# Dividing the attention output instead of the probabilities: the softmax sums sent as rows through HBM, once for each pair of heads

## The chip, the core and the metric

The kernel runs on one core of a Trainium2 chip. The metric is device time in microseconds (us) from the first to the last instruction of one execution. The engines are TensorE (PE: matmuls and transposes, with the weight loads PEld beside them), VectorE (DVE), ScalarE (ACT), GpSimd (POOL) and SyncE (SP), which here only issues DMAs. Each engine works through its own instructions strictly in order; they meet through semaphores. PE writes to eight PSUM banks; everything else lies in SBUF or in HBM.

## The reference

One layer of a hybrid backbone over 512 latent tokens with a prefix of 256 context tokens, width 1024: a modulated input projection, 16 heads of latent attention beside a two-way Mamba-2 scan (SSD), one output projection over both, then a gated MLP. What the change touches is the attention:

```python
def attend(q_nope, q_rope, k_nope, k_rope, v):
    s = (jnp.einsum("bqhd,bkhd->bhqk", q_nope, k_nope)
         + jnp.einsum("bqhr,bkr->bhqk", q_rope, k_rope)) * ATTN_SCALE
    p = jax.nn.softmax(s.astype(jnp.float32), axis=-1).astype(v.dtype)
    return jnp.einsum("bhqk,bkhd->bqhd", p, v)
...
mix_x = jnp.concatenate([attn_x, ssd_x], axis=-1) @ w_out[l]
```

Each of the 16 heads has 512 queries, 768 keys (latent and context) and values 64 wide. The softmax divides each row of exponentials by its sum; the division may stand before or behind the product with the values, since a sum belongs to one query.

## The kernel before

Every large product is done in fp32r as three products of a rounded high part and a remainder (high by high, high by low, low by high). So each operand is first split: `split` copies it on ACT to the high part (L497) and subtracts on DVE for the low part (L498). Both lines are a helper's and occur everywhere.

**Attention** goes by pairs of heads, eight of them (`pair_of_heads`). For each pair `project` makes the queries, keys and values: matmuls (L758), splits, and then eleven SBUF-to-SBUF DMAs on the SP queue that put the second head and the rotary rows on their partitions (L1156 to L1162). The value operand's low part is a POOL subtraction (L1169). For each head and each block of 128 queries `scores` makes 128 by 768 scores in PSUM (L1181), DVE takes the row maximum (L1183), ACT the exponentials with their row sums (L1185), DVE the reciprocal of the sums (L1187, one column), and POOL multiplies the 128 by 768 exponentials by it (L1188). `transposed` turns the result with six PE transposes (L1199) and splits it; `weighted` multiplies by the values (L1211). The product is added from its two halves on ACT and DVE (L1235, L1236) into `attn`, head by head: there the 64 values of a head lie on partitions and its 512 queries along the row. Two PSUM tiles (`sc`) hold scores, two or three banks (`t`) transposes.

**Beside it** the SSD runs for the first part of the attention, with its own work on all engines (L1011 to L1070, much of it POOL). **Behind it** the output projection (L1295) takes sixteen k-steps, those of the attention's eight pairs first; each weight block is loaded by SP, split on ACT and DVE. At the same time DVE makes 24 columns of modulation vectors (L586, one 512 KB weight each); when eight are done (L1275 to L1278), ACT's queue writes the vector to HBM (L1282, `mod_rows`) and reads it back as a row spread over 128 partitions (L1284). The four token blocks then go through norms (L1347 to L1379) and transposes with a modulated split (L1387, L1390, L1391) into the MLP's first products (L758 with 256 columns).

**The order** is not the code's. A planner records all instructions, prices each, works out which depend on which (PSUM banks keep the code's order), places each buffer in one of 53 blocks of SBUF, and lists each engine's instructions by rank in sixteen tries; the order of the best try by its own prices is then forced on each engine, SP included. In its prices, a DVE instruction with two SBUF operands and a POOL instruction may not run at the same time. So any edit gives a new order and new buffers for the whole program. Buffer names (`block51_52_372`) carry the block's number first.

## Time and profile before

| | us |
|---|---|
| median of 3 runs (985.85 to 990.34) | 986.82 |
| profiled execution, first to last instruction (its span) | 986.9 |
| PE busy | 964.1 |
| DVE busy | 685.7 |
| ACT busy | 500.8 |
| POOL busy | 265.0 |

The profiled execution has no time beside its span on the page; the span agrees with the median to 0.1 us, so a sum against one is a sum against the other. A busy PE is not PE at its peak, because matmuls are pipelined and their ends are modelled. The attention's scores run from about 279 to 515 us, the output projection to 607 us, the MLP from there to the end.

### The profile page before, as it was taken

The numbers are of one execution on the slowest core, as the hardware profiler recorded it, in microseconds if no ns is written. First come the engines' busy times: TensorE is split into PE (matmuls) and PEld (weight loads), VectorE is DVE, ScalarE is ACT, GpSimd is POOL, SyncE is SP. The second block draws the span as 40 slices with busy tenths as digits, with TensorE's granted clock in tenths as the row PEclk, the third lists the DMA queues.
The fourth block names the chain that finished last, engine by engine and source line by source line (L and its number), as shares of the span: only waits on it lengthen the run. The fifth ranks groups of instructions, "written<-read, shape, count | busy, mean of one in ns | idle before, by whom it ended". The sixth has DMA issues, their size and how long they took to land. (4 is left out here: it accounts for less than half of the span.)

```text
span 986.9 us, 14324 instructions
## 1 busy us (share of the span) xinstructions
PE 964.1 (98%) x5213; PEld 824.1 (84%) x5213; DVE 685.7 (69%) x1181; ACT 500.8 (51%) x996; POOL 265.0 (27%) x238
## 2 busy tenths in 40 slices
PE   8999999999999999999999998999999999999997
PEld 8888888888878878889888887988888888888885
DVE  5999877896889999878789948925244342583504
ACT  4555347548569786878786114823232242652001
POOL 0002103756599986566440001000000000000000
PEclk8999999999999999999999999999999999999999
DMA  9923211012331341334577576332222312444422
GB/s 345 376 96 114 75 43 59 23 43 62 84 98 55 105 113 36 100 96 108 149 274 272 175 155 247 129 107 86 107 86 93 120 54 75 128 144 140 144 86 106
DMA packets 47542, 121.07 MB, mean 123 GB/s; under 512 B 9057, under 2 KB 12017, under 8 KB 47473
## 3 DMA queue, kind: packets, MB, share of 16 engines
q1 hardware_dynamic: 43744, 118.49, 37.4%
q10 hardware_dynamic: 3728, 1.68, 0.6%
q8 instruction: 41, 0.67, 0.3%
q14 instruction: 29, 0.23, 0.1%
HBM read 98.11 MB, written 6.30 MB: 106 GB/s over the span
## 5 line engine op out<-in xcount | busy, mean ns | idle before, releaser
L758 PE MATMUL banks<-block,block 128*128 128x512 f32 (+1 forms) x2132 | 449.7, 362 | 4.3 <-ACT block L1390 1.9
L758 PEld LDWEIGHTS banks<-block,block 128*128 128x128 f32 x2132 | 361.8, 190 | 65.6 <-ACT block L1390 2.1
L498 DVE TENSOR_TENSOR block<-block,block 128x512 fp32r<-128x512 f32 (+5 forms) x252 | 217.8, 890 | 105.3 <-ACT block L497 44.6
L497 ACT ACTIVATE block<-block 128x512 fp32r<-128x512 f32 (+4 forms) x252 | 180.7, 746 | 204.8 <-PE banks L1482 43.0
L521 POOL TENSOR_TENSOR smalls<-smalls,powers 128x1 f32<-128x1 f32 (+3 forms) x16 | 12.7, 792 | 507.0 <-DVE smalls L1466 359.3
L1482 PE MATMUL banks<-block,block 128*128 128x512 f32 x512 | 117.8, 389 | 0.0
L1482 PEld LDWEIGHTS banks<-block,block 128*128 128x128 f32 x512 | 96.1, 188 | 19.9
L1188 POOL TENSOR_TENSOR block<-block,smalls 128x768 f32<-128x768 f32 x64 | 95.4, 1498 | 51.9 <-DVE smalls L1187 32.7
L1181 PE MATMUL banks<-block,block 128*128 128x256 f32 (+1 forms) x384 | 95.3, 355 | 5.1 <-issue 1.9
L498 DVE TENSOR_TENSOR block<-banks,block 128x512 fp32r<-128x512 f32 (+1 forms) x156 | 83.2, 556 | 13.9 <-ACT block L497 12.5
L1295 PE MATMUL banks<-block,block 128*128 128x512 f32 x384 | 89.2, 390 | 0.0
L497 ACT ACTIVATE block<-banks 128x256 fp32r<-128x256 f32 (+1 forms) x156 | 74.0, 500 | 23.3 <-PE banks L1199 10.8
L1295 PEld LDWEIGHTS banks<-block,block 128*128 128x128 f32 x384 | 71.6, 188 | 14.7 <-DVE block L1236 0.2
L1181 PEld LDWEIGHTS banks<-block,block 128*128 128x128 f32 x384 | 59.7, 189 | 13.0 <-ACT block L1185 4.4
L1211 PE MATMUL banks<-block,block 128*128 128x256 f32 x384 | 68.7, 294 | 0.1
L1185 ACT ACTIVATE block<-banks,smalls 128x768 f32<-128x768 f32 x64 | 58.0, 907 | 14.4 <-DVE smalls L1183 10.1
L1183 DVE TENSOR_REDUCE smalls<-banks 128x1 f32<-128x768 f32 x64 | 60.8, 950 | 5.9 <-PE banks L1181 5.6
L586 DVE SCALAR_TENSOR_TENSOR block<-block,block 128x1024 f32<-128x1024 f32 x50 | 60.3, 1219 | 6.2 <-DMA block<-in_wmod_dram 6.1
L1199 PE MATMUL banks<-cst,block 128*128 128x128 f32 x384 | 63.2, 273 | 0.1
L1211 PEld LDWEIGHTS banks<-block,block 128*128 128x128 f32 x384 | 56.4, 189 | 4.6 <-ACT block L497 1.1
L793 DVE SCALAR_TENSOR_TENSOR block<-banks,cwh,block 128x510 f32<-128x510 f32 (+3 forms) x88 | 51.7, 621 | 11.3 <-ACT block L789 10.5
L1199 PEld LDWEIGHTS banks<-cst,block 128*128 128x128 f32 x384 | 46.5, 140 | 8.1 <-issue 2.2
(220 smaller groups left out, 1040.8 us busy)
## 6 DMA issues: line engine op xcount, KB each, us to landing
block<-in_wmod_dram SPq DMA_DIRECT2D x48, 512.0 KB, 6.2
block<-in_wup_dram SPq DMA_DIRECT2D x44, 512.0 KB, 4.5
block<-in_wdn_dram SPq DMA_DIRECT2D x44, 256.0 KB, 3.3
block<-block SPq DMA_DIRECT2D x32, 256.0 KB, 3.0
block<-in_wout_dram SPq DMA_DIRECT2D x16, 512.0 KB, 5.2
block<-block SPq DMA_DIRECT2D x56, 128.0 KB, 2.5
block<-in_wxbc_dram SPq DMA_DIRECT2D x12, 512.0 KB, 3.3
block<-in_wz_dram SPq DMA_DIRECT2D x16, 256.0 KB, 6.0
```

Of the source, the lines that this page charges most:

```text
L497: act(hi, src, AF.Copy)
L498: (lo_eng or V).tensor_tensor(out=lo, in0=src, in1=hi, op=ALU.subtract)
L586: V.scalar_tensor_tensor(out=junk, in0=wt, scalar=0.5, in1=vec, op0=ALU.mult, op1=ALU.mult, accum_out=acc)
L758: mm(po, lhsT=wf(k, pt[0]), rhs=xf(k, pt[1]), start=(k == 0 and pt == parts[0]), stop=(k == nk - 1 and pt == parts[-1]))
L1181: mm(sc[:, o : o + n], lhsT=q_[:, x_, qi * P : (qi + 1) * P], rhs=kk[:, y_, :], start=part == 0, stop=part == 2)
L1183: V.reduce_max(nm, sc[:, :T], axis=AX.X, negate=True)
L1185: act(pe, sc[:, :T], AF.Exp, bias=nm, scale=1.0, accum_out=sm_)
L1188: G.tensor_tensor(out=pe, in0=pe, in1=sm_.to_broadcast([P, T]), op=ALU.mult)
L1199: nc.tensor.transpose((tx if c < NX else tc_)[:, o : o + P], pe[:, s_ : s_ + P], ident)
L1211: mm(po[:, half * 256 : half * 256 + 256], lhsT=vst(c), rhs=rhs, start=(part == 0 and c == 0), stop=(part == 1 and c == NKT - 1))
L1295: mm(po[i][:, nh * 512 : nh * 512 + 512], lhsT=l[lp][:, i * P : (i + 1) * P], rhs=w[wp][:, nh * 512 : nh * 512 + 512], start=(k == 0 and l ...
L1482: mm(po[i], lhsT=l[lp][:, i * P : (i + 1) * P], rhs=w[wp], start=(k == 0 and lp == 0 and wp == 0), stop=(k == NF - 1 and lp == 1))
```

## The change

`scores` no longer takes the reciprocal of a block's sums and no longer multiplies the exponentials by it: the POOL pass over 128 by 768 is gone, and the exponentials go to the transposes as they are. The sums of a pair's eight blocks (two heads by four) are written by the exponentials into eight neighbouring columns. After the pair's products there is, once for a pair: one DVE reciprocal of 128 by 8 (L1239 of the new file), one PE transpose to 8 by 128 into a `t` bank (L1241), an ACT copy of it to SBUF (L1242), a DMA to HBM (`shares`, 4 KB), two DMAs that read a head's 512 reciprocals as one row spread over its 64 partitions (128 KB each), all three on the SP queue, and one POOL multiplication of the pair's 128 by 512 outputs in place (L1248).

```diff
+    shares = nc.dram_tensor("shares", (NPAIR, 8, P), F32, kind="Internal").ap()
+
-    def scores(qkk, qi):
+    def scores(qkk, qi, sm_):
...
-        nm, sm_ = small("nm"), small("rs")
+        nm = small("nm")
         V.reduce_max(nm, sc[:, :T], axis=AX.X, negate=True)
         pe = t4(P, T)
         act(pe, sc[:, :T], AF.Exp, bias=nm, scale=1.0, accum_out=sm_)
         pfree(sc)
-        V.reciprocal(out=sm_, in_=sm_)
-        G.tensor_tensor(out=pe, in0=pe, in1=sm_.to_broadcast([P, T]), op=ALU.mult)
         return pe, ox, oc
...
-        at = attn[hp // 2][:, hp % 2, :]
+        at, sums = attn[hp // 2][:, hp % 2, :], small("rs", 8)
...
-                    transposed(*scores(heads[j], half * 2 + q2), pT, q2)
+                    qi = half * 2 + q2
+                    transposed(*scores(heads[j], qi, sums[:, j * NX + qi : j * NX + qi + 1]), pT, q2)
...
             pfree(po)
+        V.reciprocal(out=sums, in_=sums)
+        tr, row, share = pget("t"), t2(8, P), t2()
+        nc.tensor.transpose(tr[:8, :P], sums, ident)
+        act(row, tr[:8, :P], AF.Copy)
+        pfree(tr)
+        load(shares[hp], row)
+        for j in range(2):
+            load(share[j * 64 : j * 64 + 64],
+                 shares[hp, j * NX : (j + 1) * NX].rearrange("q p -> (q p)").unsqueeze(0).to_broadcast([64, S]))
+        G.tensor_tensor(out=at, in0=at, in1=share, op=ALU.mult)
```

The planner gives a new order everywhere. Three places matter below. (Lines of the new file stand up to eleven lower than those of the old.)

SP's queue in the middle of the attention. Before, it holds only the copies of `project` and its weights:

```order
L1159 DMA block1_552_3421<-block40_551_3420 32x1024
L1160 DMA block1_552_3421<-block3_199_1371 32x1024
L1156 DMA block45_654_4138<-block36_411_2582 64x1024
L489 DMA block51_609_3854<-in_wqn_dram 128x384
L1162 DMA block49_46_346<-block49_46_346 64x512
L1161 DMA block36_411_2582<-block3_199_1371 64x1024
L1156 DMA block52_619_3866<-block50_132_733 64x512
```

Now a pair's write and its two reads stand among them, here those of the third pair among the copies of a later one:

```order
L1156 DMA block16_621_3821<-block22_489_2990 64x1024
L489 DMA shares<-block51_52_372 8x128
L489 DMA block51_52_372<-shares 64x512
L1159 DMA block22_489_2990<-block23_555_3392 32x1024
L1160 DMA block22_489_2990<-block41_199_1367 32x1024
L489 DMA block51_52_372<-shares 64x512
L1156 DMA block3_385_2475<-block38_622_3822 64x1024
L1156 DMA block12_33_288<-block47_132_733 64x512
```

The first read stands right behind the write whose data it reads, so SP holds there until the write has landed, and the copies behind it wait too.

DVE behind the attention. The end of the first modulation vector before, some forty rows behind the attention's last addition (L1236); from there to L1278 stand 12 columns (L586), 13 splits of 128 by 1024 and 13 of 128 by 512 (L498), the last of which are shown:

```order
L586 SCALAR_TENSOR_TENSOR block44_779_5074,mod_98<-block15_713_4554,block4_6_87 128x1024
L586 SCALAR_TENSOR_TENSOR block38_809_5193,mod_98<-block2_808_5191,block4_6_87 128x1024
L498 TENSOR_TENSOR block15_896_5533<-block34_788_5112,block0_895_5532 128x1024
L1275 TENSOR_TENSOR mod_98<-mod_98,prm_90 128x8
L498 TENSOR_TENSOR block31_893_5528<-block28_715_4582,block7_878_5482 128x512
L1277 TENSOR_SCALAR mod_98<-mod_98 128x8
L586 SCALAR_TENSOR_TENSOR block19_646_4106,mod_98<-block41_818_5233,block4_6_87 128x1024
L1278 TENSOR_TENSOR mod_98<-mod_98,prm_90 128x8
```

Now, right behind the attention's last addition (L1237 of the new file; L1286 to L1289 are the old L1275 to L1278):

```order
L586 SCALAR_TENSOR_TENSOR block35_798_5011,mod_98<-block41_797_5009,block4_6_87 128x1024
L586 SCALAR_TENSOR_TENSOR block13_805_5045,mod_98<-block7_799_5037,block4_6_87 128x1024
L586 SCALAR_TENSOR_TENSOR block0_807_5049,mod_98<-block27_806_5047,block4_6_87 128x1024
L586 SCALAR_TENSOR_TENSOR block15_816_5087,mod_98<-block22_717_4424,block4_6_87 128x1024
L586 SCALAR_TENSOR_TENSOR block35_798_5011,mod_98<-block38_817_5113,block4_6_87 128x1024
L586 SCALAR_TENSOR_TENSOR block20_823_5122,mod_98<-block32_822_5120,block4_6_87 128x1024
L586 SCALAR_TENSOR_TENSOR block0_807_5049,mod_98<-block37_841_5198,block4_6_87 128x1024
L1286 TENSOR_TENSOR mod_98<-mod_98,prm_90 128x8
L498 TENSOR_TENSOR block20_838_5193<-block46_347_2333,block1_837_5192 128x1024
L1288 TENSOR_SCALAR mod_98<-mod_98 128x8
L498 TENSOR_TENSOR block52_696_4343<-block9_594_3681,block50_493_2993 128x512
L1289 TENSOR_TENSOR mod_98<-mod_98,prm_90 128x8
```

The first vector is finished 7 columns and 2 splits behind the attention. The second, which was 17 columns and 28 splits behind it, is now 15 columns and 22 splits behind it.

ACT's queue around the two vectors' DMAs. Before, the last split of an output weight (the last L497 ahead of L1347) stands ahead of the first read:

```order
L1282 DMA mod_rows<-mod_98 128x8x1
L497 ACTIVATE block34_900_5539<-block44_779_5074 128x1024
L1347 ACTIVATE block21_789_5114,smalls_65<-banks_64 128x1024
L1282 DMA mod_rows<-mod_98 128x8x1
L1284 DMA block2_808_5191<-mod_rows 128x1024
L497 ACTIVATE block23_935_5771<-block38_809_5193 128x1024
L1284 DMA block35_727_4691<-mod_rows 128x1024
```

Now (L1293, L1295 and L1358 are the old L1282, L1284 and L1347):

```order
L1293 DMA mod_rows<-mod_98 128x8x1
L497 ACTIVATE block15_906_5459<-block7_799_5037 128x1024
L497 ACTIVATE block13_911_5465<-block18_541_3317 128x1024
L1295 DMA block35_798_5011<-mod_rows 128x1024
L497 ACTIVATE block6_916_5473<-block51_788_4992 128x1024
L497 ACTIVATE block16_954_5708<-block7_799_5037 128x1024
L1293 DMA mod_rows<-mod_98 128x8x1
L1358 ACTIVATE block1_853_5242,smalls_65<-banks_64 128x1024
L497 ACTIVATE block28_951_5703<-block5_644_3976 128x1024
```

One split of an output weight (into block6) has moved behind the first read, which must wait for its write to land.

## The prediction

> **What bounds the kernel now.** I read the busy times first, then the chain of work that ended last, then the busy times of five stages, then what PE waited for.
>
> ```profile
> PE 964.1 (98%) x5213; PEld 824.1 (84%) x5213; DVE 685.7 (69%) x1181; ACT 500.8 (51%) x996; POOL 265.0 (27%) x238
> PE 36%; DMA 3%; DVE 2%; issue 1%; ACT 0%; POOL 0%; DVEq 0%; POOLq 0%; ACTq 0%
> ```
>
> PE is busy for all but 22.8 of 986.9 us, and the chain, which is followed back only to 559 us, is mostly PE. The rest of it is DMA and DVE, so there is one place where PE does not set the time. The stages (attention beside SSD, attention alone, output projection, the handover to the MLP, the MLP) show where:
>
> ```profile
> 283.00:400.00 117.00, 113.44 (x699) 96.62 (x698) 109.70 (x193) 93.46 (x235) 99.76 (x85) 1.00 0.29 76
> 400.00:525.00 125.00, 121.34 (x847) 108.72 (x845) 101.14 (x195) 102.68 (x220) 64.73 (x50) 1.00 0.51 149
> 525.00:607.00 82.00, 82.00 (x363) 67.77 (x362) 65.71 (x111) 21.69 (x30) 3.66 (x5) 1.00 0.72 217
> 607.00:624.00 17.00, 13.41 (x86) 12.41 (x85) 13.74 (x39) 13.52 (x35) 2.89 (x4) 0.80 0.44 163
> 624.00:974.00 350.00, 350.00 (x1657) 294.26 (x1656) 154.66 (x223) 112.17 (x169) 1.10 (x2) 1.00 0.32 109
> ```
>
> Columns are the stage, its length, the busy us of PE, PEld, DVE, ACT and POOL with their instructions, PE's granted clock, DMA share and GB/s. In the two attention stages PE idles 3.56 + 3.66 = 7.2 us. In the first of them DVE is 94% busy and POOL 85%. In the handover PE idles 3.6 us and runs at a mean clock of 0.80, another 17 x 0.20 = 3.4 us lost. The projection (82.0 us / 363 = 0.226 us a matmul) and the MLP have no hole, and nothing of the change is in the MLP. So the pool that the change can draw on is 7.2 + 7.0 = 14.2 us. Of the attention's 7.2 us, these waits are the largest:
>
> ```profile
> PE banks L1181 <- issue: 1.9, 1, 1.9
> PE banks L1181 <- ACT block L1185: 1.9, 3, 0.7
> PE banks L1181 <- DMA block<-block: 1.2, 2, 0.7
> ```
>
> Scores wait for a score tile that the exponential frees, or for queries and keys that DMAs still bring. No wait of PE for POOL's multiplication L1188 is among PE's listed waits.
>
> **The change, part by part.** What goes, and what the new instructions are priced by:
>
> ```profile
> L1188 POOL TENSOR_TENSOR block<-block,smalls 128x768 f32<-128x768 f32 x64 | 95.4, 1498 | 51.9 <-DVE smalls L1187 32.7 <-PE banks L1199 14.2 <-ACT block L497 1.7
> L1187 DVE RECIPROCAL smalls<-smalls 128x1 f32<-128x1 f32 x64 | 9.2, 155 | 8.9 <-ACT block L1185 8.3
> L1199 PE MATMUL banks<-cst,block 128*128 128x128 f32 x384 | 63.2, 273 | 0.1
> L1390 ACT ACTIVATE block<-banks,mod 128x128 fp32r<-128x128 f32 x32 | 9.7, 368 | 3.3 <-DVE block L1391 2.7 <-PE banks L1387 0.2
> L1070 POOL TENSOR_TENSOR block<-block,block 128x512 f32<-128x512 f32 x6 | 8.4, 1399 | 11.3 <-DVE block L1066 5.9 <-PE banks L758 5.4
> L1045 DVE TENSOR_TENSOR block<-block,block x32: 405/426/1684, 199.1 to 366.7; 128x256 f32<-128x256 f32 x32
> ```
>
> POOL loses 95.4 us and gains 8 multiplications of 128 by 512 at 1.4 us, 11.2 us: -84.2 us. DVE loses 9.2 us and gains 8 reciprocals, about 1.3 us if eight columns cost what one does (0.155 us): -7.9 us. The last row shows more for DVE: an addition-like instruction with two SBUF operands takes 405 ns at best and up to 1684 ns. A busy time that quadruples for the same shape is time held up while running, and it falls in the stretch where POOL is 85% busy; with less POOL work some of it goes. Neither engine is PE, so this is worth only what PE waited for because of it. Bounds: nothing, since PE never lists L1188 as a releaser, and all of the 7.2 us. Without the DMA wait and "issue" (3.1 us, the operands of the last pair) 4.1 us are due to compute engines. I take -3.0, near that, because the first stage is where DVE has no room and each score tile passes DVE, then ACT, before PE gets it back.
>
> PE gains 8 transposes. The nearest row is L1199, 128 columns too: 63.2 / 384 = 0.165 us of PE's busy time each, 0.273 us from start to end: +1.3 us, between 0 (they fall into holes) and 8 x 0.273 = 2.2. PE is the path, so they count. ACT gains 8 copies of 8 by 128; the nearest is L1390, 0.368 us: 2.9 us, hidden while ACT is idle 23.5 + 22.3 us in the two stages; if that cover fails, a `t` bank comes back that much later, 0.4 us a pair.
>
> The 24 DMAs are SP's. Nearest are a store to HBM, a load of the same buffer, and an SBUF copy of 128 KB:
>
> ```profile
> gates<-block SPq DMA_DIRECT2D x8, 256.0 KB, 2.0
> block<-gates SPq DMA_DIRECT2D x8, 256.0 KB, 3.0
> block<-block SPq DMA_DIRECT2D x56, 128.0 KB, 2.5
> 489.71 0.49 SPq L1162 DMA_DIRECT2D block<-block  x1
> 490.85 0.47 PE L1181 MATMUL banks<-block,block 128*128 128x512 f32 x1 [1.91 <-issue]
> 494.18 0.63 PE L1181 MATMUL banks<-block,block 128*128 128x256 f32 x3 [0.65 <-DMA block<-block]
> ```
>
> Issuing costs SP 24 x 0.49 = 11.8 us in all. The write takes about 2.0 us to land, the reads 2.5 to 3.0, then POOL 1.4: some 7 us from ACT's copy to the divided output. Its reader is the output projection, and the eighth pair's k-step is the eighth: 7 x 24 matmuls x 0.226 = 38 us of other products lie ahead, so the delay is covered for every pair; for the last, the split on DVE and ACT must still fit. What is queued behind the waits is the price. On SP the copies of a later pair stand behind each write-to-read wait of about 2 us. On POOL the multiplication waits for its reads, and behind it stand SSD additions and the value splits L1169; POOL is the emptiest engine afterwards, so I cost that at nothing. For SP the last three rows show what late copies do: the last pair's came behind prefetched weights, and PE lost 1.91 + 0.65 = 2.56 us at its scores. Seven later pairs could each pay that: bounds 0 and 17.9 us. I take 0: queries and keys are planned well ahead of their scores, and PE waited for them only at that place and once more for 0.5 us.
>
> The handover is where the new order matters. Its chain of waits, with DVE's and ACT's part:
>
> ```profile
> 563.79 10.08 DMA mod_rows<-mod
> 573.89 17.18 DMA block<-mod_rows
> DVE block L1360 <- DMA block<-mod_rows: 8.2, 1, 8.2
> 526.38 0.69 DVE L1236 TENSOR_TENSOR block<-banks,block 64x512 f32<-64x512 f32 x1
> L586 DVE SCALAR_TENSOR_TENSOR block<-block,block 128x1024 f32<-128x1024 f32 x50 | 60.3, 1219 | 6.2 <-DMA block<-in_wmod_dram 6.1
> L498 DVE TENSOR_TENSOR block<-block,block 128x1024 fp32r<-128x1024 f32 x77 | 93.5, 1225 | 43.7 <-PE banks L758 23.3 <-ACT block L497 18.0 <-issue 1.8
> L498 DVE TENSOR_TENSOR block<-block,block 128x512 fp32r<-128x512 f32 x150 | 109.7, 758 | 61.5 <-ACT block L497 26.6 <-PE banks L1482 25.1 <-PE banks L758 9.1
> 614.43 5.35 PE banks L758 x24
> ```
>
> DVE ended the attention at 527.1 us and finished the first vector at 563.8, 36.7 us later. Its write and spread read took 10.1 + 17.2 us, so the first token block's norm started at 591.2, after DVE had idled 8.2 us; the later blocks queued behind it, and PE's first MLP products came late and slow (24 of them in 5.35 us). In the new order 7 columns and 2 splits lie between: 7 x 1.219 + 1.225 + 0.758 = 10.5 us. The row should land some 26 us earlier, while DVE still splits weights. The second vector comes 8 us earlier: 2 x 1.219 + 3 x 1.225 + 3 x 0.758 = 8.4 us of DVE work less. Then the second row becomes the late one, with the same two DMAs to go through. Bounds: all 7.0 us of the handover's loss gone, or, where the second row or ACT's wait for its write comes late, the 8.2 us wait once more on top. I take -3.0: DVE and ACT come 8 us earlier into the chain, but the last token block's norms still start only when PE ends.
>
> The clock here: PE idled 3.6 us and the mean granted clock was 0.80. The Trainium skill (TensorE: Matmul & The Clock Gate, What's actually happening) has the clock halved after an idle window of about 3.4 us. By that rule a gap brought under the window would return the 3.4 us at once, and this term would be -3.4 - 3.0 = -6.4, the sum 978.8; I keep to the rows.
>
> Sum: 986.9 - 3.0 + 1.3 - 3.0 = **982.2 us**, 4.7 under the span and 4.6 under the median of 986.82. About 0.5% (4.9 us) is what a measurement of this kernel can tell from no change.
>
> **The rivals.**
>
> *Nothing reaches the end.* POOL and DVE are off the path, PE's small waits move elsewhere, and the second row is as late as the first was. Then only the transposes count: 986.9 + 1.3 = 988.2. For it: no wait of PE on POOL. Against: DVE at 94%.
>
> *SP's waits make the copies late.* Each pair's scores wait for copies that stand behind the write and its landing. Price 2.56 us a pair; with four of seven pairs hit, and the handover still gained, 986.9 + 1.3 + 4 x 2.56 - 3.0 = 995.4; with seven and no gain 1006. It decides from three pairs on: three give 992.9, two 990.3, within 0.5% of before. For it: eleven copies a pair stand in one queue, and SP cannot pass a wait. Against: PE lost to copies at two places only.
>
> *More room than the idle time shows.* PE waits between matmuls whose modelled ends overlap, so its busy time hides waits. By the weight loads the two attention stages have 242.0 - 96.6 - 108.7 = 36.7 us without one. If a third of it were waiting that the shorter chain saves, 986.9 - 12.2 + 1.3 - 3.0 = 973. Against: the projection, without any hole, has its weight loads busy 67.77 of 82.00 us, 83%, and the attention 85%, so most of the 36.7 us is no room. The Trainium skill (Perfetto Trace Analysis, Identifying the Most-Contended Engine) says just this: the busy share of matmuls is a poor measure of what is left, that of weight loads a good one. The projection's row bears it out here only in part.
>
> **How the numbers follow.** Chances: the forecast 0.48, with its own range 978 to 986; nothing reaches the end 0.20; SP's waits 0.22; more room 0.10. Somewhat under half of the forecast's case lies below 981.9 (0.22), which with the last rival gives faster 0.32; slower is SP's rival, 0.22; the rest 0.46. The range 975 to 993 reaches to three pairs of SP's rival; it leaves out four or more (about 0.13) and the lower part of the last rival (about 0.07).
>
> **What would show it.** Right: POOL's busy time near 181 us; DVE at least 8 us less, with L1045's longest far below 1684 ns; PE's idle time between 283 and 525 us down from 7.2 to about 4; DVE's wait for the first row gone and PE's clock in the handover nearer 1.00. Wrong: PE listed as waiting at the scores for copies in several pairs, each behind a `shares` DMA; DVE waiting for the second row, or ACT for its write with an output weight's split behind it; or PE's busy time in the attention grown by more than 2.2 us. A plan that lies worse in an untouched stage would show as holes before 283 or after 624 us; I count none.

## The result and the profile after

The changed kernel takes 976.65 us (median of 5 runs, 975.91 to 977.21), the kernel before 986.82 beside it: 0.9896 of it, 95% interval 0.988 to 0.9912, so 10.2 us faster. The profiled execution spans 974.3 us; before's spanned 986.9. In every execution with both figures on record the time is 1.7 to 1.9 us longer than the span (976.03 us for this one). So before's profiled execution took about 988.6 us, 1.8 above its median, and a sum against its span is not one against the median: of the 12.6 us between the two spans, 2.4 belong to these two executions.

The first rows of the changed kernel's page, its busy times and the chain of work that ended last:

```profile
PE 956.6 (98%) x5221; PEld 819.1 (84%) x5221; DVE 679.3 (70%) x1125; ACT 502.3 (52%) x1004; POOL 186.3 (19%) x182
PE 90%; DVE 4%; DMA 2%; issue 2%; ACT 1%; POOL 0%; SPq 0%; DVEq 0%; POOLq 0%; ACTq 0%
```

The chain now reaches back over most of the span, and the two DMAs of `mod_rows`, 10.1 and 17.2 us of it before, are not in it any more. The same five stretches as before, same columns (the stages themselves now end some 7 us earlier):

```profile
283.00:400.00 117.00, 116.32 (x758) 102.20 (x756) 103.09 (x180) 97.78 (x246) 57.20 (x58) 1.00 0.36 96
400.00:525.00 125.00, 121.71 (x816) 107.63 (x815) 102.14 (x167) 102.61 (x216) 17.13 (x18) 1.00 0.54 164
525.00:607.00 82.00, 80.39 (x373) 66.69 (x371) 65.01 (x121) 25.26 (x47) 8.70 (x10) 1.00 0.74 221
607.00:624.00 17.00, 16.88 (x142) 16.68 (x142) 16.13 (x34) 12.37 (x27) 0.00 (x0) 1.00 0.42 157
624.00:974.00 350.00, 343.49 (x1578) 286.32 (x1576) 150.18 (x216) 105.51 (x158) 2.20 (x4) 1.00 0.31 106
```

Between 283 and 525 us PE idles 0.68 + 3.29 = 3.97 us instead of 7.2, and the MLP's first products run at a clock of 1.00. PE's longest waits from the scores on:

```profile
PE banks L1183 <- DMA block<-block: 2.4, 3, 1.0
PE banks L758 <- DVE block L1402: 1.6, 3, 0.8
PE banks L1183 <- ACT block L1187: 1.0, 1, 1.0
```

L1183 are the scores (L1181 before). The tail of a pair, as it ran; the last of its rows is POOL's wait for the reads:

```profile
L1239 DVE RECIPROCAL smalls<-smalls x8: 191/201/204, 302.1 to 510.6; 128x8 f32<-128x8 f32 x8
L1241 PE MATMUL banks<-cst,smalls x8: 270/272/274, 310.9 to 515.0; 128*8 128x128 f32 x8
L1242 ACT ACTIVATE block<-banks x8: 250/251/267, 311.7 to 515.5; 8x128 f32<-8x128 f32 x8
L489 SPq DMA_DIRECT2D shares<-block x8: 292/298/434, 312.0 to 515.8; - x8
L489 SPq DMA_DIRECT2D block<-shares x16: 450/572/1186, 313.9 to 518.8; - x16
L1248 POOL TENSOR_TENSOR block<-block,block x8: 1274/1296/2256, 364.3 to 524.8; 128x512 f32<-128x512 f32 x8
  DMA block<-shares: 12.1, 2
```

These prices are near those forecast, and no wait of PE behind POOL's 12.1 us is listed.

**A measure by stage.** PE's busy time hides waits, so I compare the time that passed with dense time: each PE instruction at its steady spacing in hole-free stretches (226.5 ns for a matmul of 512 columns, 162 for 192, 118 for 256, 109 for 128, 87 for a transpose of 128 columns, and so on). What is left is called the excess. It is at most 0.3 us over the whole output projection and at most 0.4 us over the MLP's second half in every profile below, so the prices of 512 and 256 columns hold. That of a transpose is too low: where several stand between larger matmuls without a hole, the traces have 110 ns for one. At 23 ns for each of some 400 transposes, about 9 us of every attention figure below are work and not loss (21 us before, not 30), as are some 2 us ahead of it and 0.7 us of the handover. Differences between kernels change by 0.2 us, for the eight new transposes. The first z product is L685, the first large product of the program.

| excess of PE, us | before | before, second profile | after |
|---|---|---|---|
| start to the first z product | 9.9 | 8.4 | 7.0 |
| from there to the first scores | 13.2 | 13.4 | 11.5 |
| attention (first scores to last product with values) | 30.4 | 30.2 | 25.9 |
| output projection | 0.2 | 0.1 | 0.1 |
| handover, to the MLP's second half | 9.0 | 12.1 | 5.1 |
| the rest | 0.0 | 0.0 | 0.1 |

So of the 12.6 us between the two spans, 4.5 lie in the attention, 3.9 in the handover, 1.7 in the stage ahead of the attention and 2.9 in the start; the eight transposes take back 0.7 of dense time (0.9 at 110 ns each, with 4.7 for the attention), and some 0.3 lies behind the last matmul.

### The profile page after: what moved, and what is told of

The parts are those of the page before. It is cut to its first block, busy times and chain, and to the rows that moved or that the text cites. A ratio compares the mean times of both kernels' runs of the same rounds, so it can differ in the third digit from the quotient of the medians.

```text
span 974.3 us, 14182 instructions
## 1 busy us (share of the span) xinstructions
PE 956.6 (98%) x5221; PEld 819.1 (84%) x5221; DVE 679.3 (70%) x1125; ACT 502.3 (52%) x1004; POOL 186.3 (19%) x182
## 3 DMA queue, kind: packets, MB, share of 16 engines
q10 hardware_dynamic: 3728, 1.68, 0.7%
## 4 chain that ended last, share of the span: by engine, by line
PE 90%; DVE 4%; DMA 2%; issue 2%; ACT 1%; POOL 0%; SPq 0%; DVEq 0%; POOLq 0%; ACTq 0%
PE banks L758 42%; PE banks L1493 12%; PE banks L1306 8%; PE banks L1183 6%; PE banks L685 5%; PE banks L1211 4%; PE banks L1199 4%; PE banks L1115 2%; PE banks L1064 1%; PE banks L1016 1%; DVE block L498 1%; PE banks L1056 1%; DMA block<-block 1%; PE banks L596 1%; PE banks L1031 1%
## 5 line engine op out<-in xcount | busy, mean ns | idle before, releaser
L758 PE MATMUL banks<-block,block 128*128 128x512 f32 (+1 forms) x2132 | 443.9, 360 | 1.6 <-DVE block L1402 1.6
L498 DVE TENSOR_TENSOR block<-block,block 128x512 fp32r<-128x512 f32 (+5 forms) x252 | 224.2, 916 | 130.5 <-ACT block L497 62.4
L497 ACT ACTIVATE block<-block 128x512 fp32r<-128x512 f32 (+5 forms) x252 | 180.3, 743 | 201.3 <-PE banks L758 60.1
L1493 PE MATMUL banks<-block,block 128*128 128x512 f32 x504 | 117.0, 389 | 0.0
L521 POOL TENSOR_TENSOR smalls<-smalls,powers 128x1 f32<-128x1 f32 (+3 forms) x16 | 12.6, 785 | 483.8 <-DVE smalls L1477 361.1
L1183 PE MATMUL banks<-block,block 128*128 128x512 f32 (+1 forms) x384 | 95.0, 355 | 3.8 <-DMA block<-block 2.4
L498 DVE TENSOR_TENSOR block<-banks,block 128x256 fp32r<-128x256 f32 (+1 forms) x156 | 83.7, 558 | 17.4 <-ACT block L497 15.9
L1306 PE MATMUL banks<-block,block 128*128 128x512 f32 x384 | 89.7, 390 | 0.0
L497 ACT ACTIVATE block<-banks 128x256 fp32r<-128x256 f32 (+1 forms) x156 | 74.0, 496 | 24.8 <-PE banks L1199 11.2
L1211 PE MATMUL banks<-block,block 128*128 128x256 f32 x384 | 72.1, 297 | 0.5 <-DVE block L1237 0.3
L1183 PEld LDWEIGHTS banks<-block,block 128*128 128x128 f32 x384 | 59.9, 189 | 11.6 <-issue 1.8
L1187 ACT ACTIVATE block<-banks,smalls 128x768 f32<-128x768 f32 x64 | 57.9, 904 | 19.0 <-DVE smalls L1185 18.2
L1199 PE MATMUL banks<-cst,block 128*128 128x128 f32 x384 | 66.1, 273 | 0.6 <-DVE block L498 0.4
L586 DVE SCALAR_TENSOR_TENSOR block<-block,block 128x1024 f32<-128x1024 f32 x50 | 60.9, 1242 | 7.0 <-DMA block<-in_wmod_dram 6.9
L685 PE MATMUL banks<-block,block 128*128 128x512 f32 x192 | 47.6, 397 | 0.3 <-ACT block L639 0.3
```

Of the source, the lines that this page charges most:

```text
L497: act(hi, src, AF.Copy)
L498: (lo_eng or V).tensor_tensor(out=lo, in0=src, in1=hi, op=ALU.subtract)
L586: V.scalar_tensor_tensor(out=junk, in0=wt, scalar=0.5, in1=vec, op0=ALU.mult, op1=ALU.mult, accum_out=acc)
L685: mm(po[i], lhsT=hx[k][:, hp, i * P : (i + 1) * P], rhs=wz[wp], start=(k == 0 and wp == 0 and hp == 0), stop=(k == KD - 1 and hp == 1))
L758: mm(po, lhsT=wf(k, pt[0]), rhs=xf(k, pt[1]), start=(k == 0 and pt == parts[0]), stop=(k == nk - 1 and pt == parts[-1]))
L1183: mm(sc[:, o : o + n], lhsT=q_[:, x_, qi * P : (qi + 1) * P], rhs=kk[:, y_, :], start=part == 0, stop=part == 2)
```

## The experiments

Theory R: the removed pass made the attention lighter, and the handover's gain is the place of the first modulation vector. Theory P: the new plan is a lucky one. Theory S: part of the difference is the start, which varies between executions. All kernels below are timed against the kernel before on the same chip, where its median was 987.7 to 989.1 us. Here are all results. 2400 and 2600 are a planner constant in ns, 15 us and 10 us one of its prices (both shown below): each gives another plan of the same kernel. "Ahead + attention" is the excess from the first z product to the attention's last product, "held up" the time that DVE's instructions between 270 and 525 us took over the shortest one of the same line and shape, "vector" when the first modulation vector's write was issued, "wait" PE's longest single wait in the handover (us).

| kernel | time, us | ratio (95%) | ahead + attention | held up | vector | wait | handover |
|---|---|---|---|---|---|---|---|
| before | 986.82 | 1 | 13.2 + 30.4 | 28.8 | 563.8 | 1.9 | 9.0 |
| before, again | 990.13 (one run) | | 13.4 + 30.2 | 26.9 | 562.2 | 4.4 | 12.1 |
| before, 2400 | 992.47 | 1.0047 (1.0028–1.0067) | 15.1 + 34.1 | 33.2 | 561.1 | 2.7 | 9.0 |
| before, 2600 | 989.05 | 1.0013 (1.0000–1.0026) | 14.4 + 30.9 | 28.3 | 558.2 | 2.8 | 9.3 |
| before, 15 us | 980.64 | 0.9925 (0.9896–0.9954) | 16.0 + 24.9 | 25.8 | 533.0 | 1.6 | 4.4 |
| before, 2400 and 15 us | 989.59 | 1.0014 (0.9998–1.0029) | 15.3 + 34.8 | 34.5 | 542.5 | 0.2 | 4.1 |
| before with the tail added | 990.89 | 1.0023 (1.0009–1.0038) | 15.9 + 30.3 | 35.2 | 547.3 | 2.5 | 8.7 |
| after | 976.65 | 0.9896 (0.9880–0.9912) | 11.5 + 25.9 | 18.2 | 530.2 | 0.8 | 5.1 |
| after, 2400 | 984.12 | 0.9961 (0.9945–0.9976) | 13.8 + 25.4 | 13.8 | 556.2 | 3.7 | 10.8 |
| after, 2600 | 986.55 | 0.9974 (0.9960–0.9989) | 14.0 + 22.0 | 12.6 | 553.2 | 4.8 | 12.0 |
| after, 15 us | 981.97 | 0.9938 (0.9916–0.9959) | 13.7 + 29.1 | 18.1 | 529.0 | 0.5 | 3.5 |
| after, 2400 and 15 us | 976.77 | 0.9886 (0.9869–0.9903) | 11.2 + 24.8 | 11.7 | 526.3 | 0.8 | 5.1 |
| after, 2600 and 15 us | 978.69 | 0.9901 (0.9885–0.9918) | 12.3 + 26.1 | 16.0 | 522.1 | 0.6 | 5.1 |
| after, 10 us | 985.50 | 0.9962 (0.9949–0.9975) | 15.2 + 27.8 | 22.7 | 534.0 | 2.8 | 8.0 |
| after without the division | 979.83 | 0.9914 (0.9890–0.9937) | 12.2 + 25.9 | 15.7 | 556.4 | 1.5 | 5.9 |
| after, POOL pass in the chain | 994.21 | 1.0052 (1.0032–1.0072) | 12.1 + 33.5 | 31.7 | 558.7 | 7.2 | 15.3 |
| after, POOL pass off the chain | 993.11 | 1.0049 (1.0034–1.0064) | 12.8 + 32.6 | 32.2 | 561.5 | 4.2 | 12.2 |
| after, POOL memsets | 989.53 | 1.0010 (0.9995–1.0025) | 13.5 + 25.3 | 17.7 | 556.7 | 5.3 | 17.8 |
| after, POOL memsets, 2400 | 974.58 | 0.9868 (0.9849–0.9887) | 13.0 + 22.6 | 20.4 | 547.1 | 0.9 | 4.6 |
| after, DVE additions | 985.18 | 0.9992 (0.9969–1.0016) | 13.3 + 27.9 | 23.2 | 559.6 | 3.2 | 14.2 |

**The kernel before once more**, unchanged.

> The kernel before, unchanged, profiled a second time. The changed kernel's profiled execution reaches its first z matmul 2.85 us earlier (17.99 instead of 20.84 us) although the orders of all engines are the same up to there; PE's clock in the first 25 us was 0.86 before and 1.00 after. Theory S (the start differs from execution to execution, and is no part of the change): this profile reaches the first z matmul at about 18 us, and its span is near 984. Theory C (the start belongs to the compiled kernel, through its code or its data's places): 20.8 us and a low clock again, span near 987.

The first 25 us of before, of this profile and of after (same columns as above; the eighth number is PE's clock):

```profile
0.00:25.00 25.00, 21.34 (x126) 20.30 (x126) 14.22 (x35) 10.83 (x19) 2.16 (x10) 0.86 0.94 344
```

```profile
0.00:25.00 25.00, 21.22 (x134) 20.05 (x134) 15.00 (x39) 10.76 (x19) 2.16 (x10) 0.93 0.94 353
```

```profile
0.00:25.00 25.00, 21.63 (x146) 20.45 (x147) 16.40 (x40) 11.97 (x21) 2.16 (x10) 1.00 0.95 355
```

The first z product came at 19.40 us, between the two expectations, with a clock of 0.93. One kernel's start differs by 1.4 us between two executions, and over all profiles here the start's excess is 6.7 to 10.1 us. So at least half of the 2.9 us can be the execution; that all of it is was not shown. The handover differed too, by 3.1 us, and the span did not come down to 984.

**Both kernels, planned anew.** One constant of the planner, how long a buffer rests in the plan before its place is used again:

```diff
-UNITS, EDGE, MARGIN = 212, 180, 2500
+UNITS, EDGE, MARGIN = 212, 180, 2400
```

> The kernel before, with nothing changed but one planner constant (a buffer's place may be taken again 2400 instead of 2500 ns after its last use in the plan), so that order and buffers are new everywhere. Theory P (most of the 10.2 us is a luckier plan): the time moves by 4 us or more, to 977 to 983 or up to 995. Theory R (the gain comes from the removed pass over the exponentials, by way of a lighter attention): within 2 us of the kernel before, 985 to 989.

> The changed kernel with the same planner constant at 2400, so with another plan. In its order 12 columns of modulation vectors and not 7 stand on DVE between the attention's last addition and the end of the first vector, as late as in the kernel before. Theory R with the handover's gain due to the place of that vector: the attention's gain stays, the handover's 4 us go, 979 to 982, PE's clock in the handover below 0.9 again. Theory P: anything from 975 to 987, with the attention's time moved as much as the handover's. Handover's gain due to something else than the vector's place: 975 to 978.

The kernel before lost 0.47%, by a worse attention; its time says that a plan is worth 4 us, as theory P had it and against theory R's 985 to 989. The changed kernel kept its short attention (25.4) and lost 5.7 us in the handover, where the vector now comes at 556 and PE waits 3.7 us. Its time, 984.12, is just above the range that goes with the vector's place.

**The pass put back**, as a multiplication by ones in the chain:

```diff
         pfree(sc)
+        G.tensor_tensor(out=pe, in0=pe, in1=ones[:, :1].to_broadcast([P, T]), op=ALU.mult)
         return pe, ox, oc
```

> The changed kernel with POOL's pass over each block's 128 by 768 exponentials put back, as a multiplication by a column of ones; division and sums stay at the end of the pair. POOL has its 95 us back, and the way from scores to transposes its latency. Theory R: the attention's excess over dense PE work (4.5 us of the gain) comes back, DVE's additions with two SBUF operands beside SSD are long again (L1045 up to over 1600 ns), 981 to 985. Theory P, or that the gain of the attention came from the sums' reciprocals or from the order: 975 to 979, with POOL at about 280 us busy.

The attention's excess is 33.5 us, so it came back, and more; DVE is held up 31.7 us. The time is above both ranges, because the handover took 15.3.

**The same pass behind the transposes**, where it delays nobody directly, and **two memsets** in the same place, which load POOL for nearly as long but read no operand:

```diff
         pfree(tx, tc_)
+        G.tensor_tensor(out=pe, in0=pe, in1=ones[:, :1].to_broadcast([P, T]), op=ALU.mult)
```

```diff
         pfree(tx, tc_)
+        for _ in range(2):
+            G.memset(pe, 0.0)
```

> The changed kernel with POOL's pass over each block's 128 by 768 exponentials put back, but behind the transposes that read them, where nobody reads its result: POOL has the 95 us, the way from the scores to the transposes has no latency of it. Beside the run with the pass in the chain it tells what of the pass cost PE. If its latency between exponentials and transposes: attention's excess 25 to 27 us, as in the changed kernel, with POOL at 280 us busy. If its load on POOL, and the instructions of DVE with two SBUF operands that it holds up: 31 to 34. The handover (8 columns between) adds 5 to 15 us by its plan, so the whole time, 977 to 990, says less than the attention does.

> The changed kernel with two POOL memsets over each block's 128 by 768 exponentials, behind the transposes that read them and off the chain. By the memset of 128 by 192 (0.25 us) and that of 64 by 512 (0.52 us) two take about 1.5 us, as the POOL pass (1.56 us in the run with the pass off the chain), so POOL is as busy as there, 270 to 290 us, but reads nothing. Theory D (the pass costs PE because DVE's instructions with two SBUF operands are held up while POOL's read SBUF): DVE's time over the shortest of its forms between 270 and 525 us stays at 12 to 20 us, PE's excess from the first z product to the attention's last at 36 to 43. Theory Q (POOL's queue is late): DVE is not held up either, but the excess is 45 or more, with waits for POOL's SSD additions. If memsets hold DVE up too: 26 us or more held up, and 43 or more.

> The same with the planner constant at 2400, a second plan of it, since plans of one kernel differ by 3 us either way in this stage. Theory D: held up 12 to 20 us, excess 36 to 43. Theory Q: 45 or more.

With the pass off the chain, between 270 and 525 us, the groups of POOL's added work and of DVE's addition L1045, and then that stretch's busy times (columns as above):

```profile
L1204 POOL TENSOR_TENSOR block<-block,ones 128x768 f32<-128x768 f32 x64 | 99.5, 1561 | 44.5 <-PE banks L1199 36.1 <-ACT block L497 5.2 <-DMA block<-shares 1.5
L1045 DVE TENSOR_TENSOR block<-block,block 128x256 f32<-128x256 f32 x16 | 11.4, 722 | 0.0
```

```profile
270.00:525.00 255.00, 245.84 (x1598) 214.06 (x1597) 224.91 (x352) 203.99 (x473) 185.82 (x150) 0.99 0.43 122
```

The same with the memsets, in their first plan:

```profile
L1205 POOL MEMSET block<- 128x768 f32 x128 | 93.4, 741 | 39.8 <-PE banks L1199 32.9 <-ACT block L1187 4.3
L1045 DVE TENSOR_TENSOR block<-block,block 128x256 f32<-128x256 f32 x16 | 8.8, 551 | 3.9 <-POOL block L1044 3.9
```

```profile
270.00:525.00 255.00, 248.97 (x1619) 217.48 (x1618) 215.98 (x357) 205.81 (x474) 175.78 (x213) 1.00 0.45 128
```

L1045 in the same stretch before, and after:

```profile
L1045 DVE TENSOR_TENSOR block<-block,block 128x256 f32<-128x256 f32 x16 | 13.9, 872 | 0.0
```

```profile
L1045 DVE TENSOR_TENSOR block<-block,block 128x256 f32<-128x256 f32 x16 | 7.8, 490 | 3.8 <-POOL block L1044 3.8
```

The pass costs PE as much off the chain (45.4 us ahead + attention) as in it (45.6), so it is not its latency, nor the per-block reciprocals, which neither run has. With memsets POOL is nearly as busy (175.8 us against 185.8 in this stretch), and the excess is 38.8 and 35.6, as in the changed kernel: it is not POOL's busy time either. Each figure is one plan, and seven plans of the changed kernel (below) lie at 36.0 to 43.0; the two with the pass lie 2.4 us or more above them all. Off the chain the time, 993.11, is above the 977 to 990 forecast; the memsets' second plan lies 0.4 us outside both of its ranges. What goes with the excess is DVE being held up, 31.7 and 32.2 us with the pass, 17.7 and 20.4 with the memsets; the one instruction shown needs 722 ns, or 551.

The hold-up itself can be read from the traces, first in the kernel before, then with the memsets:

```profile
366.21 1.92 POOL L1188 TENSOR_TENSOR block<-block,smalls 128x768 f32<-128x768 f32 x1
366.73 1.68 DVE L1045 TENSOR_TENSOR block<-block,block 128x256 f32<-128x256 f32 x1
368.34 0.94 DVE L1183 TENSOR_REDUCE smalls<-banks 128x1 f32<-128x768 f32 x1
```

```profile
356.95 0.74 POOL L1205 MEMSET block<- 128x768 f32 x1
357.05 0.42 DVE L1045 TENSOR_TENSOR block<-block,block 128x256 f32<-128x256 f32 x1
```

L1045 needs 405 ns at its shortest. Beside the pass it takes 1.68 us, ends 0.28 us behind it, and the next row maximum (L1183 in that kernel) starts only then. Inside a memset it takes 0.42 us. I counted DVE's instructions with two `block` operands in SBUF that began at least 0.1 us before the end of a running pass: 10 of 13 before, and 15 of 20 with the pass off the chain, took over 0.1 us longer than the shortest of their form, 10.0 and 10.6 us together. Beside a running memset none of 38 in the two plans did; the worst took 0.05 us longer. So that the pass holds DVE up, and a memset does not, is shown. The Trainium skill (SBUF — State Buffer, SBUF: two separate sides) states the rule: DVE with two SBUF inputs and a GpSimd instruction that reads SBUF shut each other out for a whole instruction. These runs agree with it, the 0 of 38 beside memsets with the part on reading. The memsets' second plan is, with 94 us of useless work on POOL, the fastest kernel of the study (974.58); its interval overlaps that of the changed kernel, so that it is faster is not shown.

**DVE loaded without POOL**: one addition for each block, off the chain.

```diff
         pfree(tx, tc_)
+        V.tensor_tensor(out=pe[:, :P], in0=pe[:, :P], in1=pe[:, P : 2 * P], op=ALU.add)
```

> The changed kernel with one more DVE instruction for each block of queries, behind the transposes and off the chain: a 128 by 128 addition of two SBUF operands in the exponentials, whose result nobody reads. By the 405 ns of the 128 by 256 addition L1045 it takes about 0.22 to 0.25 us, 64 of them 14 to 16 us, as much as DVE's instructions between 270 and 525 us were held up more with POOL's pass (27 to 33 us over the shortest of their form) than without (14 to 18 us). POOL stays at some 186 us. Theory D (the pass cost PE because it held up DVE): PE's excess from the first z product to the attention's last product goes from 37.4 (39.2 and 42.8 in the changed kernel's other plans) to 43 to 47, as with the pass (43.6, 49.2, 40.9, 45.6, 45.4). Theory that POOL itself came late (its queue, its SSD additions): 37 to 41.

```profile
L1204 DVE TENSOR_TENSOR block<-block 128x128 f32<-128x128 f32 x60 | 21.6, 371 | 1.3 <-PE banks L1199 1.0
```

With 21.6 us of work more on DVE, over the 14 to 16 meant, the excess is 41.2: 0.2 above the rival's range, 1.8 below theory D's, and within the changed kernel's own plans (36.0 to 43.0). It doesn't support theory D. The runs above show that the pass costs PE and that it holds DVE up; that PE pays for it by way of DVE's lost time is argued, not shown.

**The tail without its division**, and **the tail added to the kernel before**. The first leaves out everything from the reciprocal to POOL's multiplication; the second keeps the old division and adds the tail.

```diff
-        V.reciprocal(out=sums, in_=sums)
-        tr, row, share = pget("t"), t2(8, P), t2()
...
-        G.tensor_tensor(out=at, in0=at, in1=share, op=ALU.mult)
```

```diff
         pfree(sc)
+        rs = small("rs")
+        V.reciprocal(out=rs, in_=sm_)
+        G.tensor_tensor(out=pe, in0=pe, in1=rs.to_broadcast([P, T]), op=ALU.mult)
         return pe, ox, oc
```

> The changed kernel without the division at the end of a pair: the sums are made but nothing divides by them, so the softmax's division is left out and the reciprocals, transposes, copies, DMAs and POOL multiplications of the tail are gone. What is counted is PE's time beyond the dense time of its instructions, in the attention (kernel before 30.3 us in two profiles, its new plan 34.1; changed kernel 25.9, its new plan 25.4; with the pass back 33.5) and in the handover (9.0 and 12.1; 9.0; 5.1; 10.8; 15.3). Theory R (the pass was the cost, the tail costs PE only its eight transposes): attention 24 to 26, so 0 to 1 us under the changed kernel there. Theory that the tail's waits on SP cost PE something: attention 22 or less. In its order 17 columns stand between the attention's last addition and the first vector's end, so by the theory that the vector's place sets the handover its handover is 9 or more, and the time 979 to 983.

> The kernel before, with its division kept, and the changed kernel's tail added to it: reciprocal of 128 by 8, transpose, copy, write, two reads and POOL multiplication for each pair. The output is divided twice by the softmax sums. It has everything that the change adds and nothing that it removes. Theory R: PE's excess up to the attention's last product stays at 41 to 49 us plus 1 for the transposes, the time at 985 to 995. Theory that the tail's waits on SP cost about 2.56 us at each of three or more pairs: waits of PE's scores for copies of 8 us and more, time above 996.

Without the tail the attention's excess is 25.9, the changed kernel's own: SP's waits cost PE nothing that can be seen. Added to the kernel before, the tail leaves ahead + attention at 46.2, inside the range of before's plans, and none of PE's listed waits there is for a copy. The first one's handover was forecast at 9 or more and came at 5.9 although its vector was late (556.4): the one exception to the vector's rule on that side. The second's vector came at 547.3 and its handover took 8.7, an exception on the other.

**The vector early in both kernels.** The planner's price of a column written to HBM as a row:

```diff
-DMA_START, DMA_WAIT, DMA_AHEAD, DMA_ALONE, DMA_WORDS = 650, 910, 3000, 0.8, 5000
+DMA_START, DMA_WAIT, DMA_AHEAD, DMA_ALONE, DMA_WORDS = 650, 910, 3000, 0.8, 15000
```

> The kernel before with one price of the planner changed: a column written to HBM as a row is taken to need 15 us and not 5. Its order now has 4 columns and not 11 between the attention's last addition and the end of the first modulation vector, as early as in the changed kernel; nothing of the change is in it. Theory H (the handover's gain is the vector's place in the plan and has nothing to do with the pass): handover's excess about 5 instead of 9 to 12 us, PE's clock there 1.00, attention's excess unchanged at 30 to 34, time 981 to 985. Theory that the vector's row comes as late as before because its DMAs are slow under load: 986 to 990.

> The changed kernel with the same price at 15 us: in its order no column stands between the attention's last addition and the first vector's end (7 in the changed kernel, 12 in its other plan). Theory H: handover's excess 4 to 5 us, attention's 25 to 26, time 974 to 978, no slower than the changed kernel. If plans scatter by several us for other reasons: up to 984, with the excess in another stage.

The handover fell to 4.4 and 3.5 us, so the gain goes with the vector's place, and the kernel before has it without the change. In the table, seven of the eight profiles with the write by 547.1 us have 5.1 us or less in the handover, eleven of the twelve with a later one 8.7 or more. What I had not expected: the attention moved just as far, down to 24.9 in the kernel before (with 16.0 ahead of it) and up to 29.1 in the changed one, and at this price the change makes no gain (980.64 against 981.97). Theory H had forecast 25 to 26 us of attention and 974 to 978 us for the changed kernel.

**More plans**: both constants at once, 2600 in each kernel, 2600 with 15 us, and 10 us.

> The kernel before with both planner constants changed (2400 ns, 15 us): one more plan of it, with 5 columns between the attention's last addition and the first vector's end. Theory H: handover's excess 4 to 6 us. If the pass costs PE 5 us over plans, its excess from the first z product to the attention's last is 41 to 49 and the time 980 to 990; if the plan decides all, it may be as low as 975.

> The changed kernel with both planner constants changed: one more plan of it, 2 columns between. Theory H: handover's excess 3.5 to 6 us. Excess from the first z product to the attention's last 37 to 43, time 973 to 982, and 3 us or more under the kernel before with the same constants; if the plan decides all, no such difference.

> The kernel before with the planner constant at 2600: one more plan of it, with 10 columns between the attention's last addition and the first vector's end. Excess from the first z product to the attention's last 41 to 50 (43.6, 49.2, 40.9, 50.1 so far), handover 9 or more, time 984 to 994.

> The changed kernel with the planner constant at 2600: one more plan of it, with 10 columns between. Excess from the first z product to the attention's last 36 to 43 (37.4, 39.2, 42.8, 36.0 so far), handover 9 or more by the vector's place, time 979 to 986; 3 us or more under the kernel before at the same constant.

> The changed kernel with the buffer constant at 2600 ns and the price of a column written as a row at 15 us; no column between the attention's last addition and the first vector's end. Theory H: first vector written before 547 us, handover's excess 3.5 to 6 us. Excess from the first z product to the attention's last 36 to 43. If both come at their best, 970 to 975, under the changed kernel's 976.65; otherwise up to 982.

> The changed kernel with the price of a column written as a row at 10 us; 3 columns between. Theory H: first vector written before 547 us, handover's excess 3.5 to 6 us. Excess from the first z product to the attention's last 36 to 43, DVE held up between 270 and 525 us for 12 to 20 us, time 972 to 982.

PE's longest wait in the handover and the busy times of 605 to 625 us, first in the kernel before with both constants, then in the changed kernel at 2600:

```profile
PE banks L758 <- ACT block L1390: 0.2, 1, 0.2
```

```profile
605.00:625.00 20.00, 19.65 (x126) 17.11 (x125) 17.90 (x47) 12.17 (x37) 2.93 (x4) 1.00 0.34 119
```

```profile
PE banks L758 <- ACT block L1401: 4.8, 1, 4.8
```

```profile
605.00:625.00 20.00, 17.50 (x127) 16.92 (x128) 18.47 (x50) 16.70 (x42) 2.33 (x3) 0.83 0.33 108
```

Four forecasts held in time (before with both constants, before at 2600, after with both constants, after at 2600 and 15 us), two did not: after at 2600 came 0.6 us above its range and only 2.5 us under its partner, and after at 10 us came 3.5 above, with the vector early and a handover of 8.0, where DVE waited 2.6 us for the second vector's row, and with 22.7 us of DVE held up instead of 12 to 20. The excess ahead and in the attention left its range twice, by 1 us each: 50.1 in the kernel before and 36.0 in the changed one, both with both constants. The hoped-for sum of short attention and early vector did not appear: the plan that joined both constants gave 26.1 and 5.1, and 978.69 us.

Taken together: five plans of the kernel before lie at 0.9925 to 1.0047 of its time, mean 1.0000; seven of the changed kernel at 0.9886 to 0.9974, mean 0.9931. Over plans the change is worth 0.69%, 6.8 us (with so few plans the 95% interval of this mean is 1 to 12 us), and it lies ahead of the attention's end: ahead + attention is 45.8 on average before and 39.0 after (the transposes take 0.7 back), the handover 7.2 and 7.1 (before's second profile left out). The ranges overlap, so one plan against one plan can show no gain, or 13 us (989.59 and 976.77 with both constants).

## Why the prediction was right or wrong

It said 982.2 us, a gain of 4.6 to 4.7; measured are 10.2. The time lies in its range, near the lower end, and the gain is more than twice as large. The sum was made against the profiled span, and that fell by 12.6 us, 7.9 more than the sum says: at the table's prices 2.9 in the start, 1.7 ahead of the attention, 1.5 in the attention, 0.9 in the handover, 0.6 of transposes and 0.3 behind the last matmul. So one term was sized too small, and nothing stood for two stages. Part is luck: over plans the change is worth 6.8 us, and with 0.9896 this plan is the second best of seven. By its steps:

- *Attention −3.0* is the step that was sized wrong. PE's idle time did fall to the 4 us forecast (3.97), but the excess fell by 4.5 here, and by 5.1 over plans (31.0 to 25.9). The pool was taken as PE's idle time of 7.2 us; what PE lost against dense time in the attention was three times that, some 21 us with transposes at 110 ns. The cause was seen, L1045's quadrupled time beside a busy POOL, but it was costed by PE's list of waits, where this loss does not show.
- *PE's transposes +1.3*: 0.7 at the table's price, 0.9 at 110 ns each, within the bounds.
- *SP's waits 0*: right. PE's waits at the scores for copies are 2.4 us in three places, 1.2 in two before. The rival with 2.56 us a pair did not occur in any of the kernels with the tail. (Of those 2.56 us the profile puts 1.91 down to issue and only 0.65 to a copy.)
- *Handover −3.0*: right in mechanism and nearly in size, −3.9 (−7.0 against before's second profile). The first vector's write is issued at 530.15 us, read back from 545.30, and DVE takes it up at 561.49 without a wait:

```profile
530.15 0.39 ACTq L1293 DMA_DIRECT2D mod_rows<-mod  x1
545.30 0.36 ACTq L1295 DMA_DIRECT2D block<-mod_rows  x1
561.49 1.23 DVE L1371 TENSOR_TENSOR block<-banks,block 128x1024 f32<-128x1024 f32 x1
```

 The gain belongs to this plan and not to the division: over plans the handover is the same in both kernels. That the second vector becomes the late one, the rival's mechanism, was seen at 10 us. The clock did come back to 1.00, but PE's longest single wait there had been 1.9 us before. By the rule of the Trainium skill (TensorE: Matmul & The Clock Gate, What's actually happening), an idle window of about 3.4 us, the term would have been −6.4 and the sum 978.8, nearer to the time; yet before's profile had no gap of that length that could be brought under it.
- *No term* stood for the start (−2.9 between the profiles) and for the stage ahead of the attention (−1.7). The first varies between executions, by half of that at least. The second goes by plan, 13.2 to 16.0 before and 11.2 to 15.2 after; what the change has to do with it stays open. "A plan that lies worse in an untouched stage" was thought of, one that lies better was not.
- *More room than the idle time shows* was the rival nearest in kind: a busy PE hid waits. Its size, a third of the time without a weight load, was too much for the changed kernel's plan. *Nothing reaches the end* is refuted.
- Signs: POOL 186.3 us against "near 181", DVE 6.4 us less and not 8, L1045's longest 1259 ns, which is not far below 1684; its mean beside the scores fell from 872 to 490 ns, which was the better thing to name.

## What to carry to other kernels

Where DVE is nearly full and POOL works beside it, look at how far instructions of one line and shape spread in time: a POOL pass that reads SBUF costs DVE time that no list of PE's waits shows, and moving it off the chain did not help here. Size such a gain by PE's time over its dense time in the stage, not by PE's idle time, and take the price of every shape, transposes too, from a stretch without holes. Where a planner orders everything anew, compare several plans on both sides before saying what an edit is worth; here plans of the kernel before lay from 7 us under it to 5 us over, as much as the edit was worth.

## What the runs showed that was not expected

- PE's clock in the handover fell with single waits of about 2 us. In the six profiles with a longest wait of up to 0.9 us it stayed at 1.00; in all twelve with 1.9 us or more the worst 5 us were granted 0.50 to 0.66; with 1.6 us it stayed (before at 15 us), with 1.5 us it fell to 0.66 (after without the division). The handover's excess is 3.5 to 5.9 us in the eight profiles up to 1.6 us and 8.0 to 17.8 in the others: a step. The Trainium skill (TensorE: Matmul & The Clock Gate, What's actually happening) has the clock halved after an idle window of about 3.4 us. The single waits here need not be that long, perhaps because PE is thinly used around them, which no run tells apart.
- The same kernel's handover took 9.0 and 12.1 us in two executions: the row of the first vector came late by 8.2 and 10.8 us of DVE's waiting.
- Memsets on POOL left DVE's two-operand instructions alone (0 of 38 lengthened), while a multiplication, as long as two of them, held them up (15 of 20).
